# Sixteen experts' weights in loads of 16 KB per partition from the third expert's second product on

## The chip, the cores and the metric

The kernel runs on one core of a Trainium2 chip. The metric is the device time of one execution in microseconds (us). TensorE is called PE, VectorE DVE, ScalarE ACT, GpSimd POOL, and SyncE SP; SP issues nearly all loads. The on-chip memory has 128 partitions, and a load is described by its bytes per partition: a float32 tile of 128x2048 is 8 KB per partition, 1 MB in all.

## The reference

One layer works on 512 latent tokens and 256 context tokens of width 1024. Its first half (neighbourhood attention, a gated scan, an output projection) is not touched. The second half is a mixture of 16 experts, each of which takes the 64 tokens that it scores highest:

```python
gate, idx = lax.top_k(jnp.swapaxes(aff, 1, 2), cap)          # 16 experts x 64 tokens
xs = jax.vmap(lambda hb, ib: hb[ib])(h, idx)
hid = (jax.nn.silu(jnp.einsum('becd,edf->becf', xs, w_gate))
       * jnp.einsum('becd,edf->becf', xs, w_up))             # 1024 -> 2752
y = jnp.einsum('becf,efd->becd', hid, w_down) * gate[..., None]   # 2752 -> 1024
# y is added back to its tokens' rows; then an RMS norm, a gate, the residual
```

Each expert has three float32 matrices of 1024x2752, 33.8 MB together, each read once: 541 MB of the 602 MB that the kernel moves.

## The kernel before

The first half ends at about 377 us; then the experts run one after the other. An expert's **first product** (line 1415, PSUM tile `mm`) goes over six chunks of columns: five of 512 and one of 192. A chunk of 512 takes four loads of 1 MB, gate and up for the first and second four of eight k rows of 128; PE multiplies gate and up in turn (16 matmuls, each two records in the trace), then ACT and DVE form silu(gate)*up, and four transposes (line 1395) bring the chunk before into `hidT`. The last chunk takes two loads of 768 KB (line 1406). The **second product** (line 1444, PSUM tile `o`) takes ten loads of 1 MB, two f rows of 128 each, and one of 768 KB (line 1437). So an expert has 30 loads of 1 MB and 3 of 768 KB. The last expert's second product (`down_last`, lines 1468 to 1482) goes by three pieces of columns (512, 256, 256), so that the final norm can begin early.

Beside this stand side tasks, written as generators that `tick()` moves on: choosing and gathering tokens for the next pair of experts (`select`), and adding a pair's result to the output rows (`scatter`, line 1498: two matmuls and a DVE addition per tick, two ticks behind each chunk).

Order: instructions stand on each engine in the order of the program text. SP issues a load when its buffer is free and when the load issued eight before has landed (eight DMA semaphores, seen as `DMAHW0` to `DMAHW7` in the order below); a load that waits holds up all behind it.

Buffers: the `heap` has 18 slots of 8 KB per partition. In the expert part they are shared by weights, residual rows (`res`, two slots), accumulated rows (`acc`, two), `room` (one-hot matrices and gathered tokens, one or two) and `yy` (one). Up to fourteen of the heap's slots and five beside it (`wk` x2, `wx` x3) take weights; `weight()` picks the slot that was used longest ago, and `taken()` and `given()` keep its count. A slot is free again when PE has run its last matmul on it:

```python
if beside[0][0] < heap_free[0]:      # a slot beside the heap is older
    tag = beside.pop(0)[1]
...
heap_free.pop(0)
return big(shape, name)
```

## Time and profile before

| | |
|---|---|
| median of three runs | 1742.58 us (1741.87 to 1742.91) |
| profiled execution | 1744.71 us |
| its span | 1742.9 us |
| mean granted PE clock | 0.989 |
| PE, DVE, ACT, POOL busy | 1588.3, 549.7, 329.7, 183.9 us |
| moved by DMA | 602.45 MB, mean 346 GB/s |

The profile is of one execution; its span is the time from the first to the last recorded instruction. Slices are a fortieth of it, 43.6 us each. "Waits" are idle times of an engine, with what ended them; the "chain" follows the work that ended last backward to what released it. Matmuls overlap in the records, so a busy PE can still have room.

### The profile page before, as it was taken

The page shows a single profiled execution, that of the slowest core. Times are in us where ns is not written, and L with a number is a line of the kernel's source. Part 1 is how long each engine was busy: PE and PEld are TensorE (multiplying, and loading weights), DVE is VectorE, ACT ScalarE, POOL GpSimd, SP SyncE. Part 2 cuts the span into 40 slices and gives each one's busy share as a digit, 9 for nine tenths or more (in the row PEclk, how much of TensorE's full clock was granted, in tenths as well). Part 3 has the DMA queues.
Part 4 walks back from the last instruction along what each step waited for, and adds up shares of the span by engine and source line. Part 5 has one row for each costly group of instructions (what it writes and reads, how often), then busy time and mean ns, then how long its engine had stood idle before and what let it go on. Part 6 is the DMA issues. An engine that isn't in the chain of part 4 may idle for free.

```text
span 1742.9 us, 21564 instructions
## 1 busy us (share of the span) xinstructions
PE 1588.3 (91%) x8876; PEld 825.3 (47%) x8876; DVE 549.7 (32%) x1133; ACT 329.7 (19%) x644; POOL 183.9 (11%) x291
## 2 busy tenths in 40 slices
PE   6999999998999998989898889989998988899897
PEld 5988789776533432423243234324232423343233
DVE  4788664656513021111201120211112111302123
ACT  4463541466310100100010001001000100010002
POOL 1264254422000000000000000000000000000003
PEclk9999999999999999999999999999999999999998
DMA  9462302424899999999999999999999999999995
GB/s 384 151 237 99 121 25 88 158 74 167 342 395 421 421 421 420 420 421 421 421 421 421 420 421 421 421 421 420 421 420 421 420 421 420 421 421 420 421 421 225
DMA packets 91059, 602.45 MB, mean 346 GB/s; under 512 B 12992, under 2 KB 13888, under 8 KB 23888
## 3 DMA queue, kind: packets, MB, share of 16 engines
q1 hardware_dynamic: 90176, 598.73, 83.7%
q0 software_dynamic: 784, 2.34, 0.4%
q8 instruction: 70, 1.15, 0.3%
q14 instruction: 29, 0.24, 0.0%
HBM read 598.10 MB, written 3.16 MB: 345 GB/s over the span
## 4 chain that ended last, share of the span: by engine, by line
DMA 61%; PE 31%; DVE 4%; ACT 2%; issue 1%; POOL 1%; SPq 0%; POOLq 0%; ACTq 0%; DVEq 0%
DMA w_down<-in_w_dn_dram 15%; DMA w_up<-in_w_gu_dram 13%; DMA w_gate<-in_w_gu_dram 10%; DMA wx<-in_w_gu_dram 10%; PE mm L1415 7%; PE mm L455 6%; DMA wk<-in_w_gu_dram 4%; DMA wx<-in_w_dn_dram 4%; PE mm L466 3%; PE o L1444 2%; DMA wk<-in_w_dn_dram 2%; PE mm L824 2%; DMA wraw<-in_w_in_dram 1%; PE o L1482 1%; PE aux L1273 1%
## 5 line engine op out<-in xcount | busy, mean ns | idle before, releaser
L1415 PE MATMUL mm<-w_gate,room 128*64 128x512 f32 (+1 forms) x1056 | 422.0, 546 | 11.8 <-DVE sl L1424 10.5
L1415 PE MATMUL mm<-w_up,room 128*64 128x512 f32 (+1 forms) x960 | 396.4, 560 | 37.8 <-DMA w_up<-in_w_gu_dram 37.8
L1444 PE MATMUL o<-w_down,hidT 128*64 128x512 f32 x960 | 220.3, 598 | 12.3 <-DMA w_down<-in_w_dn_dram 11.7
L1396 DVE COPY hidT<-aux 128x256 f32<-128x256 f32 x96 | 38.7, 403 | 560.8 <-PE aux L1395 560.8
L1415 PE MATMUL mm<-wx,room 128*64 128x512 f32 (+1 forms) x584 | 197.1, 576 | 11.4 <-DMA wx<-in_w_gu_dram 11.4
L1415 PEld LDWEIGHTS mm<-w_gate,room 128*64 128x64 f32 x1056 | 137.2, 137 | 145.1 <-issue 112.0
L1415 PEld LDWEIGHTS mm<-w_up,room 128*64 128x64 f32 x960 | 124.0, 137 | 168.6 <-issue 90.3
L1420 ACT ACTIVATE sl<-mm 64x512 f32<-64x512 f32 x96 | 52.4, 546 | 743.3 <-PE aux L1395 611.4
L1415 PE MATMUL mm<-wk,room 128*64 128x512 f32 (+1 forms) x472 | 167.2, 547 | 10.8 <-DMA wk<-in_w_gu_dram 8.8
L1444 PEld LDWEIGHTS o<-w_down,hidT 128*64 128x64 f32 x960 | 63.7, 136 | 148.7 <-issue 110.2
L1346 POOL COPY hot<-room 128x256 f32<-128x256 f32 x2 | 0.9, 494 | 1047.6 <-DVE room L1248 1047.6
L1424 DVE TENSOR_TENSOR sl<-sl,mm 64x512 f32<-64x512 f32 x96 | 60.9, 634 | 144.1 <-ACT sl L1420 143.6
L1493 DVE SCALAR_TENSOR_TENSOR yy<-o,gt,yy 64x512 fp32r<-64x512 f32 x30 | 22.5, 749 | 257.9 <-ACT yy L1492 239.0
L455 PE MATMUL mm<-hl,whi 128*128 128x512 f32 x320 | 103.7, 404 | 0.0
L1415 PEld LDWEIGHTS mm<-wx,room 128*64 128x64 f32 x584 | 60.1, 136 | 91.2 <-issue 64.5
L1492 ACT ACTIVATE yy<-o,gt 64x512 fp32r<-64x512 f32 x30 | 20.5, 682 | 331.0 <-PE o L1444 271.3
L1415 PEld LDWEIGHTS mm<-wk,room 128*64 128x64 f32 x472 | 54.7, 139 | 57.7 <-issue 35.5
L455 PEld LDWEIGHTS mm<-hl,whi 128*128 128x128 f32 x320 | 59.3, 192 | 11.1 <-ACT wohi L808 0.3
L1498 PE MATMUL mm<-yy,back 128*128 128x512 f32 (+1 forms) x128 | 46.8, 447 | 18.2 <-DVE sl L1424 18.2
L455 PE MATMUL mm<-hl,wlo 128*128 128x512 f32 x160 | 63.1, 395 | 0.0
L1395 PEld LDWEIGHTS aux<-cc,sl 64*128 64x128 f32 x352 | 28.9, 137 | 69.4 <-issue 50.7
L1444 PE MATMUL o<-wx,hidT 128*64 128x512 f32 (+1 forms) x232 | 55.4, 601 | 4.7 <-DMA wx<-in_w_dn_dram 4.6
(346 smaller groups left out, 2064.0 us busy)
## 6 DMA issues: line engine op xcount, KB each, us to landing
w_down<-in_w_dn_dram SPq DMA_DIRECT2D x113, 1024.0 KB
w_gate<-in_w_gu_dram SPq DMA_DIRECT2D x106, 1024.0 KB
w_up<-in_w_gu_dram SPq DMA_DIRECT2D x102, 1024.0 KB
wx<-in_w_gu_dram SPq DMA_DIRECT2D x67, 1024.0 KB
wk<-in_w_gu_dram SPq DMA_DIRECT2D x45, 1024.0 KB
wm<-in_w_mod_dram SPq DMA_DIRECT2D x24, 1024.0 KB
wx<-in_w_dn_dram SPq DMA_DIRECT2D x24, 1024.0 KB
wraw<-in_w_in_dram SPq DMA_DIRECT2D x16, 1024.0 KB
```

Source lines behind the costliest of these rows:

```text
L455: T.matmul(p, w[wx][:, k, a], hT(hx, k, t0, t1), start=(n == 0), stop=(n == 3 * KT - 1))
L466: T.matmul(p, hT(hx, k, t0, t0 + 128), w[wx][:, k, :], start=(n == 0), stop=(n == 3 * KT - 1))
L824: T.matmul(p, lhs[lx][:, 2 * k2 + k], w[k2][wx][:, k, n * 512:(n + 1) * 512], start=(m == 0), stop=(m == 11))
L1395: T.transpose(pT[:, f], sl[:, f * 128:f * 128 + 128], ident[0:64, 0:64])
L1396: V.tensor_copy(hid[:, f0:f0 + nf], pT[:, 0:nf])
L1415: T.matmul(p[64 * g:64 * g + 64, 0:n], xe[k], ws[g][k // 4][:, k % 4, 0:n], start=(k == 0), stop=(k == KT - 1))
L1420: S.activation(sl[:, 0:n], p[0:64, 0:n], AF.Silu)
L1424: V.tensor_mul(sl[:, 0:n], sl[:, 0:n], p[64:128, 0:n])
L1444: T.matmul(pd[64 * g:64 * g + 64], hid[r, f0 + f], ww[r], start=(f0 + f == 0), stop=(f0 + f == 21))
L1492: S.activation(dst[0], src, AF.Copy, scale=gate_)
L1493: V.scalar_tensor_tensor(dst[1], src, gate_, dst[0].bitcast(F32), op0=OP.mult, op1=OP.subtract)
L1498: T.matmul(p, back[:, j * 128:(j + 1) * 128], yn[i], start=(i == 0), stop=(i == 1))
```

## The change

Until the third expert (e = 2) has finished its first product, the weights still come in the heap's slots of 8 KB, read as halves of 16 KB rows, now all 18 of them: `wk` and `wx` are gone, `res` moves to the pool `keep`, `acc`, `hot` and `xT` to the pool `mp`. Then `take_over()` closes the heap and opens nine pools of 16 KB per partition in its room. Pool 4 (`few`) holds `yy`, `hot2`, `back2`, `g2` and `yl`; the other eight take weights in turn (in the last expert seven, since `o` takes one). From there a load is 2 MB: gate and up for four k rows, or four f rows of the second product; the last chunk's gate and up come in one load of 1.5 MB. `layout()` lays the weights out in DRAM to match: a load's 16 KB per partition are contiguous. The matmuls are the same; the last expert's `tick()` calls, once per load, now stand after every fourth f row.

SP's list of loads, expert 2's second product and the start of expert 3. `w_dn` and `w_gu` are the two products' weights; the last number is float32 per partition. Before:

```order
L1434 DMA w_down<-in_w_dn_dram 128x2048 [waits DMAHW6_49,PE_49]
L1434 DMA w_down<-in_w_dn_dram 128x2048 [waits DMAHW7_49,PE_49]
L1434 DMA w_down<-in_w_dn_dram 128x2048 [waits DMAHW0_49,PE_49]
L1437 DMA wx<-in_w_dn_dram 128x1536 [waits DMAHW1_49,PE_49]
L1410 DMA wx<-in_w_gu_dram 128x2048 [waits DMAHW2_49,PE_49]
L1410 DMA wx<-in_w_gu_dram 128x2048 [waits DMAHW3_49,PE_49]
L1410 DMA wk<-in_w_gu_dram 128x2048 [waits DMAHW4_49,PE_49]
L1410 DMA wk<-in_w_gu_dram 128x2048 [waits DMAHW5_49,PE_49]
```

Changed:

```order
L1458 DMA w_down<-in_w_dn_dram 128x4096 [waits DMAHW2_49,PE_49]
L1458 DMA w_down<-in_w_dn_dram 128x4096 [waits DMAHW3_49,PE_49]
L1452 DMA w_down<-in_w_dn_dram 128x1536 [waits DMAHW4_49,PE_49]
L1404 DMA w_gu<-in_w_gu_dram 128x4096 [waits DMAHW5_49,DVE_49,PE_49]
L1404 DMA w_gu<-in_w_gu_dram 128x4096 [waits DMAHW6_49,PE_49]
L1404 DMA w_gu<-in_w_gu_dram 128x4096 [waits DMAHW7_49,PE_49]
L1404 DMA w_gu<-in_w_gu_dram 128x4096 [waits DMAHW0_49,PE_49]
```

From here on, ten loads of 1 MB become five of 2 MB in a second product, twenty become ten in a first, and two of 768 KB one of 1.5 MB: 33 loads per expert become 17. Each still waits for the load issued eight before. In all SP issues 396 DMAs instead of 609: 5 fewer in expert 2, 16 fewer in each of experts 3 to 14, 16 in the last.

The end of SP's list, from the last chunk of the last expert's first product; `w_dl` is its second product by pieces. Before:

```order
L1406 DMA w_gate<-in_w_gu_dram 128x1536 [waits DMAHW3_49,PE_49]
L1406 DMA w_up<-in_w_gu_dram 128x1536 [waits DMAHW4_49,PE_49]
L1468 DMA w_down<-in_w_dl_dram 128x2048 [waits DMAHW5_49,PE_49]
L1468 DMA w_down<-in_w_dl_dram 128x2048 [waits DMAHW6_49,PE_49]
L1468 DMA w_down<-in_w_dl_dram 128x2048 [waits DMAHW7_49,PE_49]
L1468 DMA w_down<-in_w_dl_dram 128x2048 [waits DMAHW0_49,PE_49]
L1468 DMA w_down<-in_w_dl_dram 128x2048 [waits DMAHW1_49,PE_49]
L1472 DMA w_down<-in_w_dl_dram 128x768 [waits DMAHW2_49,PE_49]
L1468 DMA w_down<-in_w_dl_dram 128x2048 [waits DMAHW3_49,PE_49]
L1468 DMA w_down<-in_w_dl_dram 128x2048 [waits DMAHW4_49,PE_49]
L1468 DMA w_down<-in_w_dl_dram 128x1408 [waits DMAHW5_49,PE_49]
L1468 DMA w_down<-in_w_dl_dram 128x2048 [waits DMAHW6_49,PE_49]
```

Changed, from the last 2 MB load of the first product:

```order
L1404 DMA w_gu<-in_w_gu_dram 128x4096 [waits DMAHW4_49,PE_49]
L1391 DMA w_gu_9412<-in_w_gu_dram 128x3072 [waits DMAHW5_49,PE_49]
L1495 DMA w_down<-in_w_dl_dram 128x4096 [waits DMAHW6_49,PE_49]
L1495 DMA w_down<-in_w_dl_dram 128x4096 [waits DMAHW7_49,PE_49]
L1495 DMA w_down<-in_w_dl_dram 128x2816 [waits DMAHW0_49,PE_49]
L1495 DMA w_down<-in_w_dl_dram 128x4096 [waits DMAHW1_49,PE_49]
L1495 DMA w_down<-in_w_dl_dram 128x1408 [waits DMAHW2_49,PE_49]
L1495 DMA w_down<-in_w_dl_dram 128x4096 [waits DMAHW3_49,PE_49]
L1495 DMA w_down<-in_w_dl_dram 128x1408 [waits DMAHW4_49,PE_49]
```

The twelve `w_dl` loads become seven; the first two carry eight f rows each, where before each carried four.

PE's list behind the last chunk (`aux<-cc,sl` are transposes, `o<-w_down,hidT` the second product, `aux<-acc,cc` part of the final sums). Before:

```order
L1395 MATMUL aux<-cc,sl 128x64 x4
L1482 MATMUL o<-w_down,hidT 64x512 x8
L1395 MATMUL aux<-cc,sl 128x64 x2
L1557 MATMUL aux<-acc_5240,cc 128x256
L1482 MATMUL o<-w_down,hidT 64x512 x4
L1557 MATMUL aux<-acc_5240,cc 128x256
```

Changed:

```order
L1422 MATMUL aux<-cc,sl 128x64 x4
L1506 MATMUL o<-w_down,hidT 64x512 x8
L1422 MATMUL aux<-cc,sl 128x64 x2
L1574 MATMUL aux<-acc,cc 128x256
L1506 MATMUL o<-w_down,hidT 64x512 x4
L1574 MATMUL aux<-acc,cc 128x256
```

The order of PE's work is the same here, though the first eight matmuls now stand on one load instead of two.

The diff, without bare context lines:

```diff
--- before.py
+++ after.py
@@ -119,6 +119,7 @@
+    cst_cm, cst = pool("cst", side="left")
@@ -161,7 +162,6 @@
-    cst_cm, cst = pool("cst", side="left")
@@ -956,7 +956,7 @@
-    res2 = [big((128, 2, D), f"res{i}") for i in range(2)]
+    res2 = [keep.tile([128, 2, D], F32, name=f"res{i}") for i in range(2)]
@@ -1237,6 +1237,31 @@
+    places, few, free = [], None, [1, 6, 7, 5, 0, 8, 2, 3]
+    def take_over():
+        nonlocal few
+        drain()
+        close(heap_cm)
+        places.extend(pool(f"place{i}", side="left") for i in range(9))
+        few = places[4][1]
+    def place(name):
+        n = free.pop(0)
+        return places[n][1].tile([128, 4096], F32, name=name, tag="place"), n
+    def weight(name):
+        w, n = place(name)
+        free.append(n)
+        return w
+    def results():
+        shape = [128, 2, 2, 512]
+        return few.tile(shape, F32R, name="yy", tag="yy") if places else big(shape, "yy", F32R)
@@ -1252,9 +1277,8 @@
-        room = big((128, 2048), "room")
-        hot = room[:, 0:1024].rearrange("p (j i c) -> p j i c", j=8, i=2)
-        xT = room[:, 1024:2048].rearrange("p (k i c) -> p k i c", k=KT, i=2)
+        hot = mp.tile([128, 8, 2, CAP], F32, name="hot", bufs=1)
+        xT = mp.tile([128, KT, 2, CAP], F32, name="xT", bufs=2)
@@ -1341,10 +1365,10 @@
-            hot2 = big((128, 4, 2, CAP), "hot2")
+            hot2 = few.tile([128, 4, 2, CAP], F32, name="hot2")
...
-            back2 = big((128, 512), "back2", F32R)
+            back2 = few.tile([128, 512], F32R, name="back2")
@@ -1359,29 +1383,32 @@
-    count = [0]
-    heap_free = [-1] * 14
-    beside = [(-3, "wk"), (-2, "wk"), (0, "wx"), (0, "wx"), (0, "wx")]
-    def weight(shape, name):
-        i = count[0] = count[0] + 1
-        if beside[0][0] < heap_free[0]:
-            tag = beside.pop(0)[1]
-            beside.append((i, tag))
-            if tag == "wk":
-                return keep.tile(list(shape), F32, name=tag, bufs=2)
-            return mp.tile(list(shape), F32, name=tag, bufs=3)
-        heap_free.pop(0)
-        heap_free.append(i)
-        return big(shape, name)
-    def taken(n=1):
-        del heap_free[:n]
-    def given():
-        heap_free.append(count[0])
+    def gate_up(e, ci, n):
+        if n < 256:
+            if places:
+                w = weight("w_gu2")[:, 0:2 * KT * n]
+                nc.sync.dma_start(w, I["w_gu2"][e])
+                w = [w[:, 0:KT * n], w[:, KT * n:2 * KT * n]]
+            else:
+                w = [big((128, KT * n), "w_gu2") for _ in range(2)]
+                for m in range(2):
+                    nc.sync.dma_start(w[m], I["w_gu2"][e][:, m * KT * n:(m + 1) * KT * n])
+            w = [a.rearrange("p (k c) -> p k c", k=KT) for a in w]
+            return [[a[:, 4 * k4:4 * k4 + 4] for a in w] for k4 in range(2)]
+        ws = []
+        for k4 in range(2):
+            src = I["w_gu"][e, ci, k4]
+            if places:
+                w = weight("w_gu")
+                nc.sync.dma_start(w, src)
+                w = [w[:, 0:2048], w[:, 2048:4096]]
+            else:
+                w = [big((128, 2048), "w_gu") for _ in range(2)]
+                for m in range(2):
+                    nc.sync.dma_start(w[m], src[:, 2048 * m:2048 * m + 2048])
+            ws.append([a.rearrange("p (k c) -> p k c", k=4) for a in w])
+        return ws
@@ -1397,22 +1424,11 @@
-            ws = [], []
-            for k4, m_ in ((0, 0), (0, 1), (1, 0), (1, 1)):
-                nm, t = ("w_gate", "w_up")[m_], ws[m_]
-                if n < 256:
-                    if k4 == 0:
-                        w = weight((128, KT, n), nm)
-                        nc.sync.dma_start(w, I["w_gu2"][e, m_])
-                        t += [w[:, 0:4], w[:, 4:8]]
-                else:
-                    w = weight((128, 4, 512), nm)
-                    nc.sync.dma_start(w, I["w_gu"][e, ci, m_, k4])
-                    t.append(w)
+            ws = gate_up(e, ci, n)
...
-                    T.matmul(p[64 * g:64 * g + 64, 0:n], xe[k], ws[g][k // 4][:, k % 4, 0:n],
+                    T.matmul(p[64 * g:64 * g + 64, 0:n], xe[k], ws[k // 4][g][:, k % 4],
@@ -1428,13 +1444,21 @@
+        if e == 2:
+            take_over()
...
-            w = weight((128, 2, D), "w_down")
-            if f0 < 20:
-                nc.sync.dma_start(w, I["w_dn"][e, f0 // 2])
-            else:
-                w = w.rearrange("p k c -> p (k c)")[:, 0:1536]
+            if f0 == 20:
+                w = weight("w_down")[:, 0:1536] if places else big((128, 1536), "w_down")
...
+            elif not places:
+                w = big((128, 2, D), "w_down")
+                nc.sync.dma_start(w.rearrange("p k c -> p (k c)"), I["w_dn"][e, f0 // 4][:, 1024 * (f0 % 4):1024 * (f0 % 4) + 2048])
+            elif f0 % 4 == 0:
+                w4 = weight("w_down")
+                nc.sync.dma_start(w4, I["w_dn"][e, f0 // 4])
+                w4 = w4.rearrange("p (k c) -> p k c", k=4)
+            if places and f0 < 20:
+                w = w4[:, f0 % 4:f0 % 4 + 2]
@@ -1448,6 +1472,9 @@
+        if i == 0:
+            yy.append(results())
+        yy = yy[0]
@@ -1460,16 +1487,13 @@
-            step = 2048 // nc_
+            step = 4096 // nc_
...
-                m, end = (f1 - f0) * nc_, f1 == 20 and nc_ < 512
-                w = big((128, 2048), "w_down")
-                nc.sync.dma_start(w[:, 0:m + end * nc_ * 3 // 2], I[f"w_dl{q}"][:, f0 * nc_:f1 * nc_ + end * nc_ * 3 // 2])
+                m, end = (f1 - f0) * nc_, nc_ * 3 // 2 * (f1 == 20)
+                w = weight("w_down")
+                nc.sync.dma_start(w[:, 0:m + end], I[f"w_dl{q}"][:, f0 * nc_:f1 * nc_ + end])
...
-                if f1 == 20 and not end:
-                    ends_ = big((128, 2048), "w_down")
-                    nc.sync.dma_start(ends_[:, 0:nc_ * 3 // 2], I[f"w_dl{q}"][:, 20 * nc_:20 * nc_ + nc_ * 3 // 2])
@@ -1480,11 +1504,12 @@
-                if q == 0 and f0 == 4:
-                    turn(*late)
-                    drain()
-                    side.append(preload())
-                tick(1 + (q > 0))
+                    if q == 0 and f == 7:
+                        turn(*late)
+                        drain()
+                        side.append(preload())
+                    if f % 4 == 3:
+                        tick(1 + (q > 0 and f % 8 == 7))
@@ -1501,8 +1526,8 @@
-            acc2 = [big((128, 2, D), f"acc{i}") for i in range(2)]
-            acc.extend(acc2[j // 2][:, j % 2] for j in range(4))
+            all_ = mp.tile([128, 4, D], F32, name="acc")
+            acc.extend(all_[:, j] for j in range(4))
@@ -1520,34 +1545,26 @@
-        yy = big((128, 2, 2, 512), "yy", F32R)
+        yy = []
...
-        if e0:
-            given()
-        taken()
...
-            taken()
...
-            given()
-            if e0 == 0:
-                taken(2)
-            side.append(scatter(e0, back, yy))
-    side.append(scatter(NE - 2, back, yy, slice(0, CAP)))
+            side.append(scatter(e0, back, yy[0]))
+    side.append(scatter(NE - 2, back, yy[0], slice(0, CAP)))
...
-    g2 = big((128, 2, D), "g2")[:, 0]
+    g2 = few.tile([128, D], F32, name="g2")
...
-    o = big((128, 2, D), "o0"), big((128, 2, D), "o1")
-    o = [o[j // 2][:, j % 2] for j in range(4)]
-    yl = big((128, 2, D), "yl", F32R)
+    o = place("o")[0].rearrange("p (j c) -> p j c", j=4)
+    o = [o[:, j] for j in range(4)]
+    yl = few.tile([128, 2, D], F32R, name="yl", tag="yy")
@@ -1628,9 +1646,9 @@
-    w_gu = tiles(gu[..., :2560].reshape(NE, 2, 2, 4, 128, 5, 512), 0, 5, 1, 2, 4, 3, 6)
-    w_gu2 = tiles(gu[..., 2560:].reshape(NE, 2, 8, 128, 192), 0, 1, 3, 2, 4)
-    w_dn = tiles(w_down[:, :2560].reshape(NE, 10, 2, 128, D), 0, 1, 3, 2, 4)
+    w_gu = tiles(gu[..., :2560].reshape(NE, 2, 2, 4, 128, 5, 512), 0, 5, 2, 4, 1, 3, 6).reshape(NE, 5, 2, 128, 4096)
+    w_gu2 = tiles(gu[..., 2560:].reshape(NE, 2, 8, 128, 192), 0, 3, 1, 2, 4).reshape(NE, 128, 3072)
+    w_dn = tiles(w_down[:, :2560].reshape(NE, 5, 4, 128, D), 0, 1, 3, 2, 4).reshape(NE, 5, 128, 4096)
```

## Rows read from the trace of the kernel before

**Rows 1.** The page, part 2: GB/s moved in 40 equal slices of the span.
```profile
GB/s 384 151 237 99 121 25 88 158 74 167 342 395 421 421 421 420 420 421 421 421 421 421 420 421 421 421 421 420 421 420 421 420 421 420 421 421 420 421 421 225
```

**Rows 2.** The page, part 4: shares of the chain that ended last, by engine.
```profile
DMA 61%; PE 31%; DVE 4%; ACT 2%; issue 1%; POOL 1%; SPq 0%; POOLq 0%; ACTq 0%; DVEq 0%
```

**Rows 3.** SP's queue: start us, us, issue; last spacing behind a shorter load.
```profile
1218.05 0.33 SPq L1437 DMA_DIRECT2D wk<-in_w_dn_dram  x1
1220.49 0.33 SPq L1410 DMA_DIRECT2D w_gate<-in_w_gu_dram  x1
...
1235.44 0.33 SPq L1410 DMA_DIRECT2D w_gate<-in_w_gu_dram  x1
1237.33 0.33 SPq L1410 DMA_DIRECT2D w_up<-in_w_gu_dram  x1
```

**Rows 4.** SP's queue, the last of the 39 such places.
```profile
1639.59 0.33 SPq L1410 DMA_DIRECT2D w_up<-in_w_gu_dram  x1
1641.48 0.33 SPq L1410 DMA_DIRECT2D w_gate<-in_w_gu_dram  x1
```

**Rows 5.** All DMA packets in 700 to 1600 us.
```profile
DMA packets 53144, 378.65 MB, mean 421 GB/s; under 512 B 5901, under 2 KB 5901, under 8 KB 10125
```

**Rows 6.** The chain: one load, start and us from issue to landing.
```profile
1589.74 19.83 DMA wk<-in_w_gu_dram
```

**Rows 7.** Stretches: start:end us, PE, PEld, DVE, ACT, POOL busy, PEclk, DMA share, GB/s.
```profile
298.00:302.00 4.00, 4.00 (x36) 4.00 (x35) 2.59 (x7) 0.00 (x0) 1.79 (x5) 1.00 1.03 434
316.00:318.00 2.00, 2.00 (x11) 1.65 (x10) 0.89 (x1) 0.37 (x1) 0.00 (x0) 1.00 1.02 373
700.00:1600.00 900.00, 812.42 (x4102) 322.84 (x4103) 161.84 (x331) 73.85 (x144) 0.93 (x2) 1.00 1.01 421
1645.00:1650.00 5.00, 3.34 (x8) 0.96 (x10) 0.94 (x2) 0.68 (x1) 0.00 (x0) 0.67 1.01 418
```

**Rows 8.** The page, part 3: queue, packets, MB, share of 16 engines.
```profile
q8 instruction: 70, 1.15, 0.3%
```

**Rows 9.** The chain: PE's first-product chunk when nothing is late.
```profile
718.86 7.02 PE mm L1415 x32
```

**Rows 10.** The chain in the last expert, behind one such chunk.
```profile
1686.15 0.40 PE aux L1395 x4
...
1686.58 0.60 ACT sl L1420
...
1687.20 0.70 DVE sl L1424
...
1687.94 0.73 PE mm L1498 x2
```

**Rows 11.** PE's timeline, second product: idle and its releaser in brackets.
```profile
1626.86 1.94 PE L1444 MATMUL o<-w_down,hidT 128*64 128x512 f32 x8 [0.54 <-DMA w_down<-in_w_dn_dram]
```

**Rows 12.** PE's timeline, first product, expert in mid-run.
```profile
1005.08 3.65 PE L1415 MATMUL mm<-wx,room 128*64 128x512 f32 x14 [1.33 <-DMA wx<-in_w_gu_dram]
```

**Rows 13.** PE's timeline, first product, before the granted clock fell.
```profile
1647.73 6.08 PE L1415 MATMUL mm<-wk,room 128*64 128x512 f32 x13 [1.42 <-DMA wk<-in_w_gu_dram]
```

**Rows 14.** SP's queue, the first experts' loads.
```profile
450.41 4.63 SPq L1410 DMA_DIRECT2D wx<-in_w_gu_dram  x3
470.26 0.33 SPq L1410 DMA_DIRECT2D wk<-in_w_gu_dram  x1
...
506.97 3.76 SPq L1410 DMA_DIRECT2D wx<-in_w_gu_dram  x3
```

**Rows 15.** SP's queue, the last expert's second product.
```profile
1692.48 0.33 SPq L1472 DMA_DIRECT2D w_down<-in_w_dl_dram  x1
```

**Rows 16.** The chain, same place: PE's second product.
```profile
1701.11 3.58 PE o L1482 x16
...
1705.59 1.87 PE o L1482 x8
```

More of the change, by code (lines that the diff above doesn't have):

```diff
@@ L1599, in moe_block @@
         nc.sync.dma_start(out[rows, b], o[j][:, b])
+    for cm, _ in reversed(places):
+        close(cm)
     close(m_cm)
@@ L1602, in moe_block @@
     close(cst_cm)
-    close(heap_cm)
 def layout(x, c, ctx, c_ctx, w_mod, b_mod, g_pre1, g_post1, g_pre2, g_post2, w_in, w_out, na_rpb,
```

## Prediction

> **What bounds the kernel now.** The first view to read is the line of GB/s [rows 1]: from the slice that begins at 523 us to the last but one it stands at 420 or 421, while before that it swings between 25 and 395. So the expert part moves bytes at one steady rate for some 1200 us. The second is the chain's shares [rows 2]: DMA 61%, PE 31%. PE is busy for 812 of the 900 us from 700 to 1600 [rows 7], but it waits in both products, and for the load's landing: 0.54 us before a second product's 1 MB [rows 11], 1.33 us inside a first product [rows 12]. The third is SP's queue: a load is issued when the one eight before it has landed, and takes 19.8 us itself [rows 6], eight times the spacing. There are always eight loads queued, so the spacing of SP's issues is the time that the DMA engines take for one load, and no issue is late. What the kernel costs here is bytes by rate, and something per load.
>
> **What a load costs beside its bytes.** Behind a 1 MB load the spacing is 14.95/6 = 2.49 us (1220.49 to 1235.44); the next issue, at 1237.33, waits for the 768 KB load of 1218.05 and comes after 1.89 us [rows 3]. Of 39 such places, the last of them [rows 4], also 1.89 us, 35 lie between 1.82 and 1.94 us; medians over all are 1.884 us behind 768 KB and 2.487 us behind 1 MB. A quarter of the bytes is worth 0.603 us, all of them 4 x 0.603 = 2.412, and 2.487 - 2.412 = **0.075 us per load** remain that don't grow with the bytes. A spacing off by 0.01 us moves this by 0.04. Something of the kind is seen in the packets too: from 700 to 1600 us 5901 are under 512 B, 16 for each of 369 loads [rows 5], beside the 128 of the data. Either these or a price of each data packet would be the 0.075 us; a load of twice the bytes has as many of both, with 16 KB in a data packet where 8 KB stood, if a row of a load stays one packet, as it does now.
>
> **Part by part.**
> 1. *2 MB loads.* SP issues 213 loads fewer for the same bytes. At 0.075 us each, all on the path (DMA is the bound throughout): -16.0 us.
>    The bounds. Upwards: 2 KB per partition moved at 373 GB/s, at 316 us [rows 7], which is 0.703 us for 128 rows; 8 KB at 421 take 2.491; the difference over three is 0.596 us per 2 KB, leaving 0.107 us per load, so 213 x 0.107 = 22.8 us. I take the other value, since it comes from the very loads that are changed. Downwards: if the price belongs to each 8 KB and stays, 0. Below nothing, if 16 KB in one packet moves slower; against that stands the one larger packet in the trace, 8.5 KB per partition (`rpb`), in whose 4 us 434 GB/s were moved, at 298 us [rows 7].
>    The trace moves 421 GB/s with one core reading. The Trainium skill (DMA: Bandwidth & Descriptors, "Where 436 GB/s comes from") holds that between HBM and SBUF the HBM's side binds, at about 358 GB/s, where merging loads would give nothing; measured, 421 is over that, so this rule doesn't hold here. Its other number, 435 GB/s at the engines' ports, would make the most that a merge can give 4.98 - 4.82 = 0.16 us, an estimate, or 34 us in all.
> 2. *Buffers.* Nine places of 16 KB stand where 18 slots of 8 KB did; eight take weights. Load n waits for PE's end with load n-8, which is also the load whose landing it waits for anyway, and PE follows a landing by some microseconds at most (its idle time ends with the landing [rows 11 to 13]). As eight loads in flight and eight places are the same eight, a place is not free when its load lands but when PE has used it: SP issues later than before by the time PE needs, a 2 MB load's 16 records, 3.5 us (half of [rows 9]). Seven loads, 34 us of transfer, are then still queued. The engines don't run dry: 0 us. At the last expert seven places leave 29 us: 0.
> 3. *The first experts.* Before, three `wx` buffers take loads at 450.41 that the heap has no slot for; then SP waits until 470.26, and again until 506.97, for PE [rows 14]. Changed, 18 slots stand against 19 there; `res` leaves two slots of the heap to the loads until `yy` and the weights need them, but the 19th load waits for PE's first use at about 470, and DMA may run dry for some 2 to 4 us. It is given back at 507, where the load that PE releases sets the pace in both kernels: 0, at most one load, +2.5 us.
> 4. *take_over().* Its first place covers slots whose weights were loaded 13 MB earlier, and PE is done with them; the side tasks that its `drain()` runs are over by then (nine ticks of twelve): 0.
> 5. *PE.* Its work is the same. A chunk of the first product needs 7.02 us when fed [rows 9]; with the serial steps behind it, 0.40 + 0.60 + 0.70 + 0.73 us [rows 10] and some 0.1 of gaps, 9.55. Its 4 MB arrive in 4 x 2.49 = 9.96 us before and in 2 x 4.905 = 9.81 changed. DMA stays the bound, with 0.26 us left where 0.41 were. The last chunk of an expert, with 192 columns, gives some more room. In the second product PE waits 0.54 us per 1 MB [rows 11] and then about 1.0 per 2 MB. Cost 0; without this cover, the third rival.
> 6. *The tail.* The last 1 MB load of the first product lands at 1692.48, where the issue that waits for it stands [rows 15]; PE begins the second product at 1701.11, 8.63 us later, and comes to its ninth f row at 1705.59, 13.11 us later [rows 16]. Changed, 1.5 MB (3.70 us) and 2 MB (4.91) land 8.6 us behind that point, in time; the next 2 MB at 13.5, 0.4 us late; the rest lands ahead of PE. Cost +0.4 us, and up to 2 if the engines' ends spread more.
>
> Sum: -16.0 + 0.4 = -15.6 us. The profiled execution of 1744.71 us (span 1742.9 and 1.8 around it) would become 1729.1; it ran 2.1 us above the median of 1742.58, which becomes **1727.0 us**.
>
> **Rivals.**
> - *Nothing in it:* the price goes by 8 KB, a 16 KB row being moved as two packets of the old size, and only the small packets are saved. For it: no row shows 16 KB in a weight's packet. Against it: 8.5 KB ran at 434 GB/s [rows 7]. 1739 to 1743 us.
> - *A smaller price:* the 0.075 us rest on a spacing of 1.884; at 1.895, within what single places show [rows 3, 4], it is 0.03 us per load, and 213 of them 6.4 us: 1736.6. For it: the factor of 4 on a difference of two spacings. Against it: the rows at 316 us, which give more.
>   The Trainium skill (DMA: Bandwidth & Descriptors, "Why small descriptors are slow (HBM only)") puts a fixed three cycles on each packet, with 32 bytes a cycle: 259 cycles for 8 KB, 515 for 16 KB. A merge would then save 0.58% of 4.98 us, 0.029 us, and 213 of them 6.2 us, an estimate; the trace shows 0.075.
> - *PE takes it:* the chunks' 0.26 us of room go in a clock dip or a serial step and the first product is bound by PE at 9.55 to 9.9 us. For it: the margin. Against it: PE's waits stand in every chunk that isn't fed late [rows 12]. If a third to two thirds of the gain is lost, 1731 to 1738 us.
> - *Slower: long packets.* The only packets of 16 KB in the trace are the instruction queue's: 70 in 0.3% of 16 x 1742.9 us [rows 8], 1.0 to 1.4 us each (0.25 to 0.35%), while two of 8 KB take 2 x 0.31 = 0.62 us (2.49 us x 16 engines / 128). If weights went that way, 2 MB would take 8 us and the kernel some 2380 us. It decides from 0.63 us per packet up; each 1% more costs 10.6 us of the 1060 us in which such loads run (half as many loads, 4.98 us each): 2% over the old rate gives 1764 us. Against it: those packets go to another place, and a few of them wait among weights.
> - *Slower: the clock.* PE's granted clock was 0.67 from 1645 to 1650 [rows 7], behind a wait of 1.42 us [rows 13]; 0.67 lies between the two levels, 1.2 and 2.4 GHz. Longer waits in the second product (1.0 us per 2 MB) could bring more falls. At 6.1 us for 13 records where 2.9 was the time, each costs 3 to 7 us of PE, of which DMA's bound hides a part; four in an expert would cost up to 90 us. Against it: waits of 1.33 us in the first product went by without one [rows 12].
>
> **How the numbers follow.** The forecast, 0.62: 1727.0, its own range 1720 (0.107 per load) to 1734 (0.04). A larger gain yet, 0.04, below 1719. Nothing in it 0.08; a smaller price 0.09; PE 0.07; long packets 0.06; clock 0.04. The range runs from 1719 to 1742: it takes in the cases of a smaller price and of PE, and most of the case in which nothing is gained, and leaves out a larger gain and both slower cases. Of a measurement, 0.2% (3.5 us) can be told from no change. Faster: forecast, larger gain, smaller price and PE, 0.82. Same: 0.07, nearly all of the case without gain. Slower: 0.11, both mechanisms and a little for a longer dry stretch at 470 us.
>
> **What would show it.** GB/s in 700 to 1600 us should rise from 421 to about 427 (4.98 to 4.905 us per 2 MB), with about half the packets and small packets; SP's issues should stand 4.9 us apart, and a load should take about 35 to 39 us. PE's waits should be about 1 us per 2 MB in the second product, with the granted clock at 1.00. The span from the tail's landing to the end should be 50.8 us instead of 50.4. It is wrong if issues stand 4.98 us apart or more, if the packets are of the old size, if DMA's share falls below 1 behind 520 us, or if the clock falls in most experts.

## The result, and the profile after

| | before | changed |
|---|---|---|
| median | 1742.74 us (4 runs, 1741.87 to 1743.03) | 1731.61 us (4 runs, 1730.24 to 1732.72) |
| profiled execution, span | 1744.71, 1742.9 us | 1732.44, 1730.7 us |
| mean granted PE clock | 0.989 | 0.993 |

Between the medians the changed kernel is 11.1 us faster, where 15.6 were forecast. The ratio on record is 0.9928, 95% interval 0.9915 to 0.994; it isn't the quotient of the two medians (0.9936), and stands for 12.5 us. Measured again in 5 runs it was 0.9938 (0.9924 to 0.9951). Ratios below are those on record, each to the kernel before as it ran beside.

The page's GB/s in 40 slices, beside [rows 1]:

```profile
GB/s 386 151 232 110 122 25 78 169 86 171 280 411 420 418 422 425 428 425 428 426 425 427 427 425 426 428 425 428 425 426 427 425 428 425 426 427 425 427 426 212
```

The reader is to see two things. In mid-run there stand 425 to 428 where 420 and 421 stood. And the eleventh slice has 280 for 342, the twelfth 411 for 395: the first experts' loads come at other times.

The page's chain, beside [rows 2]:

```profile
PE 51%; DMA 41%; DVE 4%; ACT 2%; POOL 1%; issue 1%; POOLq 0%; SPq 0%; ACTq 0%; DVEq 0%
```

By this view alone PE would be the new bound (51% for 31%). It isn't. A load now waits until PE has left its place, so the chain, followed backward, runs through PE more often. The longest of SP's waits from 615 to 730 us shows it (line, what it waited for, us in total, times, longest):

```profile
SPq L1458 <- PE mm L1431: 34.2, 9, 5.8
```

What decides is the DMA engines' share in the windows (start:end, us, busy us of PE, PEld, DVE, ACT, POOL, PEclk, DMA share, GB/s):

```profile
450.00:500.00 50.00, 46.40 (x235) 19.64 (x235) 20.42 (x67) 10.89 (x25) 2.61 (x3) 1.00 0.94 387
500.00:520.00 20.00, 20.00 (x148) 9.34 (x146) 3.57 (x9) 2.11 (x4) 0.00 (x0) 1.00 0.99 403
560.00:620.00 60.00, 59.23 (x355) 27.02 (x352) 6.78 (x14) 7.30 (x16) 0.00 (x0) 1.00 1.01 419
620.00:660.00 40.00, 37.04 (x190) 14.22 (x190) 10.38 (x19) 2.48 (x5) 0.00 (x0) 1.00 1.02 424
700.00:1600.00 900.00, 786.86 (x4154) 310.40 (x4154) 164.33 (x335) 74.63 (x145) 0.94 (x2) 1.00 1.01 426
1645.00:1650.00 5.00, 3.92 (x18) 1.19 (x20) 0.60 (x1) 0.00 (x0) 0.00 (x0) 1.00 1.00 426
```

1.00 to 1.02 of the engines' time is in use in the windows from 560 us on, 1.01 in mid-run as before [rows 7]; 426 GB/s for 421. The granted clock from 1645 to 1650 us is 1.00 where it had been 0.67. The same windows of the kernel before, for the early part:

```profile
450.00:500.00 50.00, 46.42 (x232) 19.62 (x234) 20.10 (x66) 10.87 (x25) 2.60 (x3) 1.00 1.01 421
500.00:520.00 20.00, 20.00 (x148) 9.43 (x146) 3.68 (x9) 2.10 (x4) 0.00 (x0) 1.00 0.90 365
560.00:620.00 60.00, 59.23 (x356) 26.94 (x352) 6.99 (x14) 7.59 (x16) 0.00 (x0) 1.00 1.01 421
```

All packets from 700 to 1600 us, beside [rows 5]:

```profile
DMA packets 27763, 383.66 MB, mean 426 GB/s; under 512 B 3080, under 2 KB 3080, under 8 KB 4488
```

53144 packets became 27763, the small ones 3080 for 5901, and 383.66 MB were moved for 378.65. A 2 MB load (2.097 MB) took 900 x 2.097 / 378.65 = 4.985 us as two, and 4.919 as one: 0.065 us less.

The chain has loads of this length, beside [rows 6] (start, us from issue to landing):

```profile
1153.53 36.49 DMA w_gu<-in_w_gu_dram
```

36.5 us for 19.8: the forecast's 35 to 39. PE's timeline in mid-run, beside [rows 12] (idle time and its releaser in brackets):

```profile
1197.80 7.09 PE L1431 MATMUL mm<-w_gu,xT 128*64 128x512 f32 x32
...
1235.09 3.65 PE L1431 MATMUL mm<-w_gu,xT 128*64 128x512 f32 x16 [1.35 <-DMA w_gu<-in_w_gu_dram]
1239.98 3.65 PE L1431 MATMUL mm<-w_gu,xT 128*64 128x512 f32 x16 [1.25 <-DMA w_gu<-in_w_gu_dram]
```

Where PE has no side work before it, it still waits 1.25 to 1.35 us for a load of a first product; the chunk at 1197.80, behind side work (`aux<-hot,res`), finds its loads landed and waits for none. With DMA's share at 1.01, DMA stays the bound.

### The profile page after: what moved, and what is told of

Its sections match the earlier page's. It is cut to its first block, busy times and chain, and to the rows that moved or that the text cites. A ratio compares the mean times of both kernels' runs of the same rounds, so it can differ in the third digit from the quotient of the medians.

```text
span 1730.7 us, 21174 instructions
## 1 busy us (share of the span) xinstructions
PE 1545.4 (89%) x8876; PEld 803.6 (46%) x8876; DVE 549.5 (32%) x1133; ACT 330.4 (19%) x644; POOL 183.1 (11%) x291
## 4 chain that ended last, share of the span: by engine, by line
PE 51%; DMA 41%; DVE 4%; ACT 2%; POOL 1%; issue 1%; POOLq 0%; SPq 0%; ACTq 0%; DVEq 0%
DMA w_gu<-in_w_gu_dram 24%; PE mm L1431 16%; DMA w_down<-in_w_dn_dram 13%; PE o L1468 8%; PE mm L455 7%; PE mm L466 3%; PE aux L1297 3%; PE mm L824 2%; DMA w_down<-in_w_dl_dram 2%; PE aux L1422 1%; DMA wraw<-in_w_in_dram 1%; PE o L1506 1%; PE mm L377 1%; DVE part L487 1%; PE aux L1359 1%
## 5 line engine op out<-in xcount | busy, mean ns | idle before, releaser
L1431 PE MATMUL mm<-w_gu,xT 128*64 128x512 f32 (+1 forms) x3072 | 624.9, 553 | 89.0 <-DMA w_gu<-in_w_gu_dram 76.4
L1431 PEld LDWEIGHTS mm<-w_gu,xT 128*64 128x64 f32 x3072 | 212.5, 136 | 462.5 <-issue 294.3
L1468 PE MATMUL o<-w_down,hidT 128*64 128x512 f32 (+1 forms) x1320 | 298.5, 598 | 32.8 <-DMA w_down<-in_w_dn_dram 32.7
L1468 PEld LDWEIGHTS o<-w_down,hidT 128*64 128x64 f32 (+1 forms) x1320 | 88.2, 136 | 219.0 <-issue 156.1
L455 PEld LDWEIGHTS mm<-hl,whi 128*128 128x128 f32 x320 | 59.3, 192 | 11.1 <-ACT wohi L808 0.3
L1297 PE MATMUL aux<-hot,res 128*128 128x128 f32 x448 | 53.7, 278 | 0.0
L1297 PEld LDWEIGHTS aux<-hot,res 128*128 128x128 f32 x448 | 51.1, 192 | 0.9
L466 PE MATMUL mm<-whi,hl 128*128 128x256 f32 x256 | 49.1, 292 | 0.0
L1180 DVE SCALAR_TENSOR_TENSOR cmp<-aux,affs,bef 128x512 bf16<-128x512 f32 x60 | 45.1, 751 | 2.1
L1422 PE MATMUL aux<-cc,sl 64*128 64x64 f32 x352 | 41.9, 236 | 0.0
L487 DVE SCALAR_TENSOR_TENSOR part<-wm,sc,part 128x512 f32<-128x512 f32 x56 | 40.1, 777 | 3.5 <-DMA wm<-in_w_mod_dram 3.5
```

The costliest lines, as they stand in the source:

```text
L455: T.matmul(p, w[wx][:, k, a], hT(hx, k, t0, t1), start=(n == 0), stop=(n == 3 * KT - 1))
L466: T.matmul(p, hT(hx, k, t0, t0 + 128), w[wx][:, k, :], start=(n == 0), stop=(n == 3 * KT - 1))
L487: V.scalar_tensor_tensor(part[:, c], wm[:, c], sc32[:, k, 0:1], part[:, c], op0=OP.mult, op1=OP.add)
L1180: V.scalar_tensor_tensor(full[:, q:q + n], row[:, c0:c1], affs[:, j, e:e + 1], before[j][:, c0:c1], op0=OP.subtract, op1=OP.is_gt, accum_o ...
L1297: T.matmul(pX[:, k], res[j][:, (4 * k4 + k) * 128:(4 * k4 + k + 1) * 128], hot[:, 4 + j], start=(j == 0), stop=(j == 3))
L1422: T.transpose(pT[:, f], sl[:, f * 128:f * 128 + 128], ident[0:64, 0:64])
```

## The experiments

Two theories of the 0.065 us: **A**, each packet of data has a price besides its bytes, and there are half as many; **B**, each load has one (its semaphore packets, its issue). A packet of data is one row of one load, so these runs can't tell a fixed price of each packet from a rate that grows with the length of a row; A stands for both.

**Rows of 8 KB in loads of 2 MB.** The weights lie in DRAM in blocks of 128x2048; a load fetches two rows per partition (one of the edited lines; the second product's load and `layout()` change likewise):

```diff
-                nc.sync.dma_start(w, src)
+                nc.sync.dma_start(w.rearrange("p (m c) -> p m c", m=2), src.rearrange("m p c -> p m c"))
```

> The changed kernel, but each of its 195 loads of 2 MB fetches two rows of 8 KB per partition instead of one of 16 KB (weights laid out in DRAM in blocks of 128x2048); the number of loads, the places and the load of 1.5 MB stay. Theory A (the price belongs to each data packet): 195 x 0.065 us, the gain per merged load that the two traces show, come back, less some 0.5 us because the first experts' 8 KB rows lie side by side again: about 1744 us, 421 GB/s in mid-run. Theory B (the price belongs to each load: its semaphore packets, its issue): about 1731 us, 426 GB/s. Half of each: about 1737 us.

Measured: 1747.88 us, ratio to before 1.0026 (1.0016 to 1.0036); 420 GB/s. The gain is gone, with the loads still halved. All packets from 700 to 1600 us:

```profile
DMA packets 48788, 377.99 MB, mean 420 GB/s; under 512 B 3032, under 2 KB 3032, under 8 KB 4440
```

3032 small packets, as few as in the changed kernel, but 48788 in all. That is theory A. The time came out 4 us above the expectation. 1.2 of them the kernel before shows too: it took 1743.94 us beside this run, not 1742.74. 1.8 more come in because the two traces, this one and the changed kernel's, differ by 0.074 us per 2 MB load (below) and not by 0.065. In the profiled execution PE's granted clock fell twice in the last expert's first product as well. Windows of the first experts, and of 1670 to 1680 and 1690 to 1700 us:

```profile
520.00:620.00 100.00, 99.23 (x545) 40.54 (x542) 19.38 (x44) 10.39 (x21) 0.00 (x0) 1.00 1.01 419
1670.00:1680.00 10.00, 9.56 (x36) 3.03 (x37) 1.76 (x3) 0.00 (x0) 0.00 (x0) 0.83 1.02 420
1690.00:1700.00 10.00, 9.12 (x34) 2.92 (x35) 2.46 (x4) 0.56 (x1) 0.00 (x0) 0.83 1.01 427
```

The first row of these refutes a part of the expectation: with rows of 8 KB side by side again, the first experts still run at 419 GB/s. What the clock cost stands in PE's timeline: no chunk below waited for a load, and the first took 1.7 us more than the second. Behind them, the start and the last group of the last stretch:

```profile
1671.16 8.78 PE L1431 MATMUL mm<-w_gu,xT 128*64 128x512 f32 x32
...
1682.45 7.09 PE L1431 MATMUL mm<-w_gu,xT 128*64 128x512 f32 x32
...
1705.77 3.65 PE L1506 MATMUL o<-w_down,hidT 128*64 128x512 f32 x16
...
1735.86 1.25 PE L1599 MATMUL aux<-yl,back 128*128 128x256 f32 x8 [0.57 <-ACT yl L1517]
```

**The same rows in loads of 1 MB.**

```diff
-                nc.sync.dma_start(w, src)
+                for m in range(2):
+                    nc.sync.dma_start(w[:, 2048 * m:2048 * m + 2048], src[m])
```

> As the kernel with rows of 8 KB, but each place is filled by two loads of 1 MB: 195 loads more, the same packets of data. Theory A (price per data packet): no more than the kernel with rows of 8 KB in one load, about 1744 us. Theory B (price per load): 195 x 0.065 = 12.7 us over the changed kernel, about 1744 us, and 13 us over the kernel with one load. With half of each it is some 6 us above the kernel with one load. If it lies above 1746 us, places of 16 KB cost something that the 18 slots did not.

Measured: 1748.55 us, ratio 1.0032 (1.0019 to 1.0044), no different from the kernel with one load. All its packets from 700 to 1600 us:

```profile
DMA packets 51423, 377.64 MB, mean 420 GB/s; under 512 B 5711, under 2 KB 5711, under 8 KB 7119
```

5711 small packets for 3032, and the bytes moved differ by 0.1%. Twice the loads cost nothing that can be measured in the time, where theory B asked for 13 us: B has fallen. It is over the 1746 us at which I had set a price of the places, and so is the kernel beside it. Both lie 4 to 5 us over the kernel before, with rows of the same length. The traces show where: the last stretch (30.1 us for 28.75, 1.3 more), the first experts (0.7), and mid-run, where 377.99 and 377.64 MB were moved in 900 us for the 378.65 of the kernel before, which is 1.6 and 2.4 us. So something in the new layout costs a little in mid-run, with fewer packets than before; the runs don't show what.

**Rows of 4 KB**, four in each load (the same edit with `m=4`), and two in each 1 MB load of the first experts.

> The changed kernel with four rows of 4 KB per partition in each load of 2 MB (and two in each of the first experts' 80 loads of 1 MB). Theory A (price per data packet): 195 x 3 + 80 = 665 times 0.065 us, 43 us more: about 1775 us and some 405 to 410 GB/s in mid-run. Theory B (price per load): about 1731 us, 426 GB/s.

Measured: 1776.24 us, ratio 1.0193 (1.0177 to 1.0209): theory A's 1775. The same view:

```profile
DMA packets 89407, 368.89 MB, mean 410 GB/s; under 512 B 2968, under 2 KB 2968, under 8 KB 87961
```

A 2 MB load takes 900 x 2.097 / 368.89 = 5.116 us here, 4.993 with rows of 8 KB (377.99 MB), 4.919 with 16 KB. So 256 rows fewer save 0.123 us and the next 128 save 0.074: 0.06 and 0.07 us per 128 rows. (These three kernels differ in their rows alone; the 0.065 us between the kernel before and the changed one has the new layout's small cost in it.)

**The side work's old order** in the last expert's second product:

```diff
-                    if f % 4 == 3:
-                        tick(1 + (q > 0 and f % 8 == 7))
+                    if f < 19 and f % (8 if q else 4) == (7 if q else 3):
+                        tick(1 + (q > 0))
```

and one `tick(1 + (q > 0))` behind the last f row.

> The changed kernel with the last expert's side work where it stood before: behind every fourth f row of the first piece, two steps behind every eighth f row of the two others. Theory (the end grew by 1.8 us because PE changes more often between the second product and the side work): the stretch from the first matmul of the last second product to the last group of matmuls falls from 30.5 us to about 29, the time by about 1.4 us to 1730.2. Rival (the longer loads did it): the stretch stays at 30 to 30.5 us and the time at 1731.6; the one wait for a load that the trace shows there is 0.35 us.

Measured: 1728.38 us, ratio 0.9916 (0.9902 to 0.9929). PE's timeline of the last stretch, from the first matmul of the second product to the last group (`aux<-yl`). First the kernel before, with a group of the second piece and the side matmuls (`mm<-yl`) behind it:

```profile
1701.04 3.65 PE L1482 MATMUL o<-w_down,hidT 128*64 128x512 f32 x16
...
1714.44 1.95 PE L1482 MATMUL o<-w_down,hidT 128*64 128x256 f32 x16
1716.32 1.19 PE L1564 MATMUL mm<-yl,back 128*128 128x512 f32 x4
...
1729.79 1.25 PE L1582 MATMUL aux<-yl,back 128*128 128x256 f32 x8 [0.57 <-ACT yl L1492]
```

The changed kernel, with the group that waited for a load and the beginning of the second piece:

```profile
1687.73 3.65 PE L1506 MATMUL o<-w_down,hidT 128*64 128x512 f32 x16
...
1692.63 1.94 PE L1506 MATMUL o<-w_down,hidT 128*64 128x512 f32 x8 [0.35 <-DMA w_down<-in_w_dl_dram]
...
1701.70 1.08 PE L1506 MATMUL o<-w_down,hidT 128*64 128x256 f32 x8
1702.71 0.50 PE L1581 MATMUL mm<-yl,back 128*128 128x512 f32 x1
1703.40 0.49 PE L1581 MATMUL mm<-yl,back 128*128 128x512 f32 x1 [0.19 <-DVE yl L1518]
1703.83 1.08 PE L1506 MATMUL o<-w_down,hidT 128*64 128x256 f32 x8
...
1718.23 1.26 PE L1599 MATMUL aux<-yl,back 128*128 128x256 f32 x8 [0.57 <-ACT yl L1517]
```

With the old order:

```profile
1684.02 3.65 PE L1507 MATMUL o<-w_down,hidT 128*64 128x512 f32 x16
...
1688.92 1.94 PE L1507 MATMUL o<-w_down,hidT 128*64 128x512 f32 x8 [0.35 <-DMA w_down<-in_w_dl_dram]
...
1713.20 1.25 PE L1600 MATMUL aux<-yl,back 128*128 128x256 f32 x8 [0.57 <-ACT yl L1518]
```

From start to start these are 28.75, 30.50 and 29.18 us. The wait for a load, 0.35 us, stands in both of the latter; 1.3 us went with the order. Where 16 records stood together before, the changed kernel has two groups of 8 with side matmuls between, and a wait for DVE. The theory holds for the stretch. The time lies 3.2 us under the changed kernel's, by the ratios 2.1: more than the stretch, but the two didn't run side by side. The next run looks at that.

> The kernel with the old tick order once more, on the chip of the two others, as their reference. If its gain over the changed kernel is the 1.3 us of the last stretch, its ratio to the kernel before is 0.992 to 0.993; 0.9916, measured at first, would be 1.5 to 2 us more than that stretch explains.

Measured: 1729.97 us, ratio 0.9917 (0.9903 to 0.9931), as at first. By the ratios the gain over the changed kernel (0.9928, and 0.9938 when measured again below) is 2 to 4 us, of which the stretch explains 1.3. But executions of one kernel differ before the experts begin. The first weights' loads, in SP's queue of the changed kernel and of the same kernel run again (the second line is cut off by a shorter window):

```profile
378.98 92.41 SPq L1409 DMA_DIRECT2D w_gu<-in_w_gu_dram  x20
```

```profile
374.69 0.99 SPq L1409 DMA_DIRECT2D w_gu<-in_w_gu_dram  x2
```

4.3 us apart with the same program, and the two executions (1732.44 and 1729.95 us) 2.5. With the old order the loads start at 374.88 us, and at 375.50 in the second measurement. So the profiled executions need nothing beside the start and the stretch: the first pair, 1732.44 and 1727.41 us, is 5.0 apart, with 4.1 at the start and 1.3 in the stretch; the second, 1729.95 and 1729.56 us, is 0.4 apart, with 1.4 gained in the stretch and a start 0.8 later. The intervals of the ratios overlap too. The stretch is shown; a gain outside it is not.

**Fewer places.**

```diff
-    places, few, free = [], None, [1, 6, 7, 5, 0, 8, 2, 3]
+    places, few, free = [], None, [1, 6, 7, 5, 0]
```

> The kernel with the old tick order, but five places of 16 KB take the weights in turn instead of eight (four in the last expert). Theory (a place comes free long before its load is needed, since PE follows each landing by some 4 to 10 us): no more than 2 us slower than the kernel beside it, 426 GB/s in mid-run, while a load takes some 20 us from issue to landing instead of 35. Rival (the queue's depth carries the rate): DMA's share falls under 1 in places and the time grows by more than 5 us.

Measured: 1731.49 us, ratio 0.9921 (0.9906 to 0.9936), beside 0.9917 for the kernel with eight: 1.5 us more between the medians. 426 GB/s again, by the windows' columns as above; then one load of the chain, and the packets from 700 to 1600 us with five places and with eight:

```profile
700.00:1600.00 900.00, 788.64 (x4154) 310.75 (x4156) 163.97 (x335) 74.58 (x145) 0.84 (x2) 1.00 1.01 426
```

```profile
1009.35 20.69 DMA w_gu<-in_w_gu_dram
```

```profile
DMA packets 27718, 383.05 MB, mean 426 GB/s; under 512 B 3072, under 2 KB 3072, under 8 KB 4480
DMA packets 27766, 383.71 MB, mean 426 GB/s; under 512 B 3079, under 2 KB 3079, under 8 KB 4487
```

A load now takes 20.7 us instead of 36.5, and 0.17% less is moved (1.5 us in these 900). Eight loads in the queue are not what carries the rate; four ahead are enough, to within 0.2%.

**Rows of 32 KB.** With the old tick order, four pools of 32 KB; gate and up of a chunk come in one load, the second product in loads of 4, 4 and 2.75 MB, and before the last expert the pairs become eight places again:

```diff
+        if len(places) == 5:
+            w = weight("w_gu")
+            nc.sync.dma_start(w, I["w_gu"][e, ci])
...
+    narrow()
     o = place("o")[0].rearrange("p (j c) -> p j c", j=4)
```

> The kernel with the old tick order, but from expert 2's second product to the end of expert 14 four pools of 32 KB per partition: a chunk's gate and up in one load of 4 MB, the second product in loads of 4, 4 and 2.75 MB; 9 loads per expert instead of 17, rows of 32 KB. Before the last expert the pairs are closed and eight pools of 16 KB opened. Theory A (price per data packet, and a row stays one packet): 99 loads' rows fewer, at 0.065 to 0.08 us per 128 rows: 6.4 to 7.9 us less than the kernel with the old tick order beside it, some 429 GB/s in mid-run. First rival (rows over 16 KB are moved in more than one packet): the same time within 2 us, 426 GB/s, and more packets than rows. Second rival (three loads ahead and waits of up to 5 us for one of 4 MB are too coarse: PE's clock falls, or DMA runs dry): slower than the kernel beside it, DMA's share under 1 in mid-run.

Measured: 1724.38 us, ratio 0.988 (0.9866 to 0.9893), 5.6 us under the kernel beside it, for 6.4 to 7.9 expected. Packets, then windows:

```profile
DMA packets 14876, 386.94 MB, mean 430 GB/s; under 512 B 1646, under 2 KB 1646, under 8 KB 1646
```

```profile
620.00:660.00 40.00, 33.52 (x168) 12.90 (x168) 8.40 (x15) 2.10 (x4) 0.00 (x0) 0.96 0.96 395
660.00:700.00 40.00, 33.62 (x150) 11.00 (x146) 6.52 (x15) 1.96 (x3) 0.00 (x0) 0.96 1.01 433
700.00:1600.00 900.00, 805.43 (x4186) 332.90 (x4184) 169.68 (x348) 75.77 (x147) 0.94 (x2) 0.97 1.00 430
```

14876 packets for 27763, 430 GB/s: a row of 32 KB is still one packet, and a load's time goes on falling (900 x 2.097 / 386.94 = 4.878 us per 2 MB, 0.042 less for 64 rows fewer). Of the second rival a part is there too. PE's clock is 0.97 in the mean, and DMA's share is 0.96 from 620 to 660 us, at the change-over. The rate is 430 GB/s all the same.

**The change-over, first try.** Expert 2's second product in places of 16 KB, then four pools of 32 KB (`renew` closes the places and opens new ones):

```diff
+        if e == 3:
+            renew(4, [0, 2, 1, 3])
```

> The kernel with rows of 32 KB, which lost 3.4 us between 621 and 649 us, where its first loads of 4 MB waited for PE to finish with four old slots each. Now expert 2's second product still takes 16 KB rows in eight places, and these become four pools of 32 KB before expert 3. Theory (that stretch was the change-over, nothing that 32 KB do in mid-run): DMA's share stays at 1.00 between 620 and 660 us, 430 GB/s from 700 to 1600 us as before, and the time falls by some 3 us to a ratio of 0.986. Rival (any change of pools costs a dry stretch): 395 GB/s or less in one of the stretches of 620 to 700 us, the same time.

Measured: 1726.56 us, ratio 0.9898 (0.9884 to 0.9912): no gain. Its windows at the change-over:

```profile
620.00:660.00 40.00, 37.78 (x196) 14.47 (x196) 8.65 (x16) 2.10 (x4) 0.00 (x0) 1.00 1.01 424
660.00:700.00 40.00, 27.09 (x118) 8.64 (x114) 6.23 (x14) 1.96 (x3) 0.00 (x0) 0.87 0.91 383
```

The dry stretch went from the first window to the second, and grew. By this the rival was right. But in the program two of the eight pools held no tile; if such a pool takes no room, the first long load lay over a place filled just before. SP's waits from 615 to 730 us fit that: one load waited for the landing of a second product's load (columns as above):

```profile
SPq L1409 <- DMA w_down<-in_w_dn_dram: 15.5, 1, 15.5
```

The changed kernel beside it, as the reference on the same chip:

> The changed kernel once more, as the reference on the same chip. Its ratio to the kernel before should be 0.992 to 0.994, as measured at first; the kernel with rows of 32 KB should lie 10 to 13 us under it (6 to 8 from the rows, 1.3 from the last stretch's order, 3 from the change-over that no longer stalls counted only if it stalled here).

Measured: 1732.98 us, ratio 0.9938; the kernel with 32 KB is 6.4 us under it, not 10 to 13.

**The change-over, second try.** Six places, all used; the first long load over slots that PE left long before:

```diff
-    places, few, free = [], None, [0, 5, 6, 4, 3, 7]
+    places, few, free = [], None, [0, 5, 4, 3, 1, 2]
...
-        places.extend(pool(f"place{i}", side="left") for i in range(8))
+        places.extend(pool(f"place{i}", side="left") for i in range(6))
...
-            renew(4, [0, 2, 1, 3])
+            renew(4, [3, 2, 0, 1])
...
-    renew(8, [0, 1, 4, 5, 2, 3, 6, 7])
+    renew(8, [6, 7, 4, 5, 0, 1, 2, 3])
```

> In the second change-over, pools that had held no tile took no room, so the first pool of 32 KB lay over the place of the fifth load of expert 2's second product, and its load came only after that one's landing and use. Now six places are opened, all used, and the first pool of 32 KB lies over slots that PE left long before. Theory (the dry stretches came from which old slots the first long loads cover, not from the change-over as such): DMA's share 1.00 in 620 to 660 and in 660 to 700 us, 430 GB/s from 700 to 1600 us, 3 us under the first kernel with rows of 32 KB beside it, a ratio of 0.986. Rival (a change of pools always costs a dry stretch): the share falls under 0.97 in one of the two, no gain.

Measured: 1721.35 us, ratio 0.9871 (0.9855 to 0.9888). The same windows:

```profile
620.00:660.00 40.00, 37.78 (x196) 14.32 (x192) 8.09 (x15) 2.10 (x4) 0.00 (x0) 1.00 1.01 424
660.00:700.00 40.00, 28.86 (x124) 9.78 (x124) 11.18 (x27) 2.55 (x4) 0.00 (x0) 0.88 1.01 434
700.00:1600.00 900.00, 802.75 (x4210) 334.70 (x4206) 166.23 (x340) 75.34 (x147) 0.93 (x2) 0.97 1.00 430
```

DMA's share is 1.01 in both windows: a change of pools need not cost a dry stretch. That the old slots under the first long loads decide it fits both tries; the number of places and the orders were changed together, so no run shows which of them did it. This kernel beats both: 21 us under the one before on the same chip, and, by the ratios (0.9871 beside 0.9928 and 0.9938), some 10 under the changed one. The first kernel with 32 KB beside it:

> The first kernel with rows of 32 KB once more, as the reference on the same chip: a ratio of 0.987 to 0.989, and its dry stretch of 3.4 us between 621 and 649 us again.

Measured: 1725.18 us, ratio 0.9887 (0.987 to 0.9904), and 396 GB/s again from 620 to 660 us.

## Why the prediction was right, and where it was off

The time, its direction and its cause (a price beside the bytes, paid by DMA, which stays the bound) were right; the gain was overrated by 4.5 us of 15.6 between the medians.

- *The price.* The term was -16.0 us, from 0.075 us per load. It measured 0.065 from 700 to 1600 us, and 213 x 0.065 = 13.8 us. The reading of [rows 3, 4] was a difference of spacings times four, so 0.01 us in 0.075 is what it could not resolve. The 0.065 isn't the price alone: against the run with rows of 8 KB in the same places, longer rows save 0.074 us per 2 MB, and that run moved 0.17% less in mid-run than the kernel before, though with 48788 packets for 53144. So the price came out nearly to the digit, which is partly luck, and a small cost of the new layout, which the sum doesn't have and whose cause is open, takes some 0.01 us of it. What the reading left open, small packets or data packets, the runs decided: data packets. The rival of a price by 8 KB, with 16 KB moved as two packets, is excluded by the packet count; the smaller price, 0.03 us, by 426 GB/s. That rival was also worked out the wrong way: a spacing of 1.895 us would give 2.487 - 4 x (2.487 - 1.895) = 0.119 us; 0.03 would need one of 1.873. The Trainium skill (DMA: Bandwidth & Descriptors, "Why small descriptors are slow (HBM only)") puts three cycles on a packet, 0.029 us per merged load by the prediction's estimate from it; the traces show 0.065, and the measurement decides.
- *Long packets.* The rival is excluded: 16 KB rows run at 426, 32 KB rows at 430 GB/s. The instruction queue's packets of 1.0 to 1.4 us [rows 8] said nothing about weights. The 434 GB/s that were held against this rival [rows 7] hang on their window: from 298.5 to 301.5 us it is 421.
- *Buffers: 0.* Right for the queue: with five places, too, 426 GB/s were moved. Whether the small cost in mid-run is one of the places is open.
- *The first experts: 0.* Right, in the way described. The engines were dry for part of 450 to 500 us (0.94, 387 GB/s), and at 500 to 520 us they moved 403 GB/s for 365. The stretch from 370 to 520 us has 275 GB/s changed and 276 before.
- *Not in the sum:* from 560 to 620 us the loads of 8 KB rows ran at 419 GB/s, where 421 stood. Over the 140 us to the change-over that is 0.5%, 0.7 us. It isn't that they are read out of rows of 16 KB, since rows side by side ran no faster; the cause is open.
- *take_over: 0.* Right: share 1.02 from 620 to 660 us. It could have been otherwise: two of the kernels with 32 KB, whose pools lie otherwise, lost (424 - 395)/424 and (434 - 383)/434 of 40 us, 2.7 and 4.7 us, at their change-over.
- *PE: 0,* and the clock's rival. Right: from 700 to 1600 us the granted clock is 1.00 and DMA's share 1.01. (How that rival's "up to 90 us" follows from four falls of 3 to 7 us in each expert isn't shown.) With 32 KB the clock does fall (0.97 in the mean), and the rate still rises.
- *The tail: +0.4 us.* **This step failed.** The wait for a load was 0.35 us, as worked out. But "the rest lands ahead of PE" took PE's own work as unchanged, from the first six rows of its order; further down the side work is cut into smaller pieces. The stretch grew by 1.75 us; 1.3 of it went with the old order.

Together: -13.8 + 1.75 + 0.7 = -11.35 us, for 11.1 measured between medians and 12.3 between the two profiled executions. That it meets the medians so closely is luck: the ratio stands for 12.5 us, with an interval of 10.5 to 14.8, and the experts' start alone differs by up to 4.3 us between executions of one program.

## What to carry to other kernels

Where DMA engines are busy all the time and rows are already long, fewer and longer rows per partition still paid, from 4 to 32 KB: count the rows saved, not the loads, and take the price from the rate of a whole stretch (MB moved in 900 us) rather than from single spacings, with a run beside it that changes the rows alone. Where a change of pools comes between, look which old slots each new buffer covers, and check that it is given its place. Compare the order of an engine that sets the end down to its last row.

## What was not expected of the hardware

Rows of 4, 8, 16 and 32 KB ran at 410, 420, 426 and 430 GB/s in mid-run. The price per 128 rows saved didn't shrink on the way: 0.06, 0.07 and 0.08 us at the three steps. Twice as many loads and semaphore packets at the same rows cost nothing measurable (1747.88 and 1748.55 us). And a granted clock of 0.97 in the mean from 700 to 1600 us, with loads of 4 MB, went with the highest rate, 430 GB/s.
